# A decoder block whose activation and weight slots start at different places modulo 512 bytes

## The chip, the cores and the metric

The kernel runs on one core of a Trainium2 chip. The metric is the device time of one execution in microseconds (us). Before the change it is 3482.91 us, the median of three runs (3481.14 to 3483.26).

## The reference

One block of a hybrid decoder, 256 tokens, model width 2048, all in float32. It is cut here to what the kernel's large products compute:

```python
xn = _rms_norm(h, mix_norm_w[l])
proj = xn @ w_in[l]                       # 2048 x 26720
p_ssm, p_gdn, p_gate = jnp.split(proj, [SSM_PROJ, SSM_PROJ + GDN_PROJ], axis=-1)
y_ssm = _ssd_branch(p_ssm, ...) @ w_branch_ssm[l]      # 4096 x 2048
y_gdn = _gdn_branch(p_gdn, ...) @ w_branch_gdn[l]      # 4096 x 2048
gates = jax.nn.sigmoid(p_gate.reshape(b_, t, N_BRANCHES, D_MODEL) + gate_b[l])
mixed = gates[:, :, 0] * y_ssm + gates[:, :, 1] * y_gdn
h = h + mixed @ w_out[l]                               # 2048 x 2048
hn = _rms_norm(h, ffn_norm_w[l])
h = h + _peer_ffn(hn, peer_w_q[l], peer_sub_keys[l], peer_u[l], peer_v[l])
return _rms_norm(h, final_norm_w)
```

`_ssd_branch` and `_gdn_branch` are the two mixers, each a short convolution, gates and a chunked scan. `_peer_ffn` scores 128 x 128 single-neuron experts by product keys, takes 16 of them per head and token, and sums `gate * gelu(u . x) * v` over them.

## The kernel before

All weights pass through the core once, as a stream of 1,129 units of at most 128 x 1024 float32 values. `Stream.load` fetches a unit into one of four slots named raw, on the SP queue. `Stream.split` cuts it into two float32r parts: whi, a copy by ScalarE (line 107), and wlo, the remainder by VectorE (line 108). There are three slots for whi and three for wlo, and two units are cut ahead of the one in use.

The activations are cut in the same way into a high and a low part. They lie in the pool `act`, four slots of 16 KB per partition, all named t16 (t in the profile's rows): first x itself and its two parts xh and xl, later the sums of the branches, h and its parts hh and hl, and in the end cf, the coefficients of the expert values. yh and yl, the parts of a mixer's output, and m16 (m in the rows), the parts of the gated sum, lie in other pools, which come after the weights' slots in memory.

`product` runs one product: per chunk of 128 rows of the contraction and per block of 128 tokens three matmuls into one PSUM accumulator, high x high (line 302), high x low (line 303) and low x high (line 304). The activations are the stationary block of 128 x 128, loaded anew for each matmul, and the weights move, mostly 512 columns at a time. One product has 352 columns (`small`), one has 256. The chain of products is: the input projection tile by tile with the branch products between its tiles, the output projection, the queries of the expert layer, and `u` against all 16,384 experts. After them `mixing` (lines 1021, 1022, 1027 and 1024) multiplies the coefficients with the expert values v, 256 units of 12 matmuls, into eight accumulators, four of them named acc and four pst. All this is one fixed order, written out by the Python loops. Between the matmuls of `product`, `Background` hands out small steps of the mixers, the scoring and the gates: transpositions (line 234), small matmuls and VectorE and ScalarE work.

A float32r column is four bytes, so a stationary block takes 512 bytes of a partition, a moving half of a unit 2,048 bytes, and every chunk of a 512-column product starts a multiple of 512 bytes after its slot's start. Slots of one name follow each other without a gap, each as long as the longest tile of that name, and here all these lengths are multiples of 512.

Of the kernel before, what the change touches and what calls it, by code (L numbers as in the profile page):

```python
# [8 lines left out]
F = mybir.dt.float32  # L9
FR = mybir.dt.float32r  # L10
# [4 lines left out]
PSUM = bass.MemoryType.PSUM  # L15
DRAM = bass.MemoryType.DRAM

D = 2048
# [9 lines left out]


def in_proj_tiles():  # L30
    """Column ranges of w_in for each streamed tile, in the order in which they are used."""
    z, xs, b, c = 0, 4096, 8192, 9216
    dt = 10240
    gq, gk, gv = GDN_BASE, GDN_BASE + 2048, GDN_BASE + 4096
    gz = GDN_BASE + 8192
    bt = GDN_BASE + 12288

    def bc(g):
        return [(b + 128 * g, 128), (c + 128 * g, 128)]

    t = {"small": bc(0) + [(dt, 64), (bt, 16), (bt + 16, 16)]}
    for h in range(NH):
        t["qkv", h] = [(gq + 128 * h, 128), (gk + 128 * h, 128), (gv + 256 * h, 256)]
    for j in range(NH // 2):
        t["gz", j] = [(gz + 512 * j, 512)]
    for g in range(NG):
        t["sx", g] = [(xs + 512 * g, 512)]
        t["sz", g] = [(z + 512 * g, 512)]
    for g in (1, 3, 5):
        t["bc", g] = bc(g) + bc(g + 1)  # L50
    t["bc", 7] = bc(7)
    for i in range(2):
        for n in range(4):
            t["gate", i, n] = [(GATE_BASE + 2048 * i + 512 * n, 512)]
    return t


def schedule():
    """The order in which the weight tiles of the mixing sub-layer are used."""
    o = [("in", ("gz", 0)), ("in", "small")]  # L60
    for j in range(NH // 2):
        o.append(("in", ("qkv", 2 * j)))
        if j > 1:
            o.append(("br", "gdn", j - 2))
        o.append(("in", ("qkv", 2 * j + 1)))
        if j != 6:
            o.append(("in", ("gz", min(j + 1, 7))))
    o += [("in", ("gate", 1, 0)), ("in", ("gate", 1, 1)), ("br", "gdn", NH // 2 - 2),
          ("in", ("gate", 1, 2)), ("br", "gdn", NH // 2 - 1)]
    for g in range(NG):  # L70
        if g % 2:
            o.append(("in", ("bc", g)))
        o += [("in", ("sx", g)), ("in", ("sz", g))]
        if g:
            o.append(("br", "ssm", g - 1))
    o += [("in", ("gate", 1, 3)), ("in", ("gate", 0, 0)), ("in", ("gate", 0, 1)),
          ("br", "ssm", NG - 1), ("in", ("gate", 0, 2)), ("in", ("gate", 0, 3))]
    return o


class Stream:
    """Weights from DRAM: raw units ahead of their use, each cut into two float32r parts."""

    def __init__(self, tc, nc, ctx, units, raw_bufs, cut_bufs):
        self.nc, self.units = nc, units
# [13 lines left out]

    def split(self):  # L100
        t, n = self.raw.pop(self.ns)
        hi = self.pc.tile([128, 1024], FR, name="whi")
        lo = self.pc.tile([128, 1024], FR, name="wlo")
        step = n if self.ns else n // 2
        for c in range(0, n, step):
            s = slice(c, c + step)
            self.nc.scalar.activation(hi[:, s], t[:, s], AF.Copy)  # L107
            self.nc.vector.tensor_tensor(lo[:, s], t[:, s], hi[:, s].bitcast(F), op=OP.subtract)  # L108
        self.cut[self.ns] = (hi, lo)
        self.ns += 1  # L110
        self.load()
# [7 lines left out]


class Background:
    """Chains of small steps that run between the large products."""

    def __init__(self, cool=3):
        self.q, self.clock, self.cool = [], 0, cool
# [33 lines left out]
def block(ctx, tc, nc, I, out, dbg=None):  # L159
    cp = ctx.enter_context(tc.tile_pool(name="consts", bufs=1))  # L160
    T16 = ctx.enter_context(tc.tile_pool(name="act", bufs=4))
# [2 lines left out]
    dram = ctx.enter_context(tc.tile_pool(name="dram", bufs=1, space=DRAM))  # L164
    V, S, G, PE = nc.vector, nc.scalar, nc.gpsimd, nc.tensor

# [1 line left out]
    order = schedule()  # L168
    tiles = in_proj_tiles()
    wide = {}  # L170
    units = []
# [20 lines left out]
    for i, v in v_order:  # L192
        add_units("v", (2 * i + v) * 128 * 1024, 1, 1024)

# [1 line left out]
    def big_tile():  # L196
        return big.tile([128, 512], F, name="acc")

    def ps_tile():
        return psp.tile([128, 512], F, name="pst")  # L200

    half = cp.tile([128, 2], F, name="half")
# [12 lines left out]
    scb, snw, gnw = cols[:, 448:496], cols[:, 496:528], cols[:, 528:530]  # L215
    rows = cp.tile([128, 240], F, name="rows")

    xs = T16.tile([128, 2, D], F, name="t16")
    strm = Stream(tc, nc, ctx, units, 4, 3)
    first = ExitStack()  # L220
    xt = first.enter_context(tc.tile_pool(name="first", bufs=1)).tile([128, 16, T], F, name="xt")
# [8 lines left out]
    def power(dst, src, which, n):  # L230
        G.tensor_tensor(dst, src, half[:, which:which + 1].to_broadcast([128, n]), op=OP.pow)

    def tr(dst, src):
        PE.transpose(dst, src, ident)  # L234

# [1 line left out]
    def row_scale(r, m, parts):  # L237
        """m = sum of squares / D + eps, r = m ** -1/2, [128, 2] each"""
        V.tensor_reduce(m, parts, axis=mybir.AxisListType.X, op=OP.add)
        V.tensor_scalar(m, m, 1.0 / D, EPS, op0=OP.mult, op1=OP.add)  # L240
        power(r, m, 0, 2)
# [45 lines left out]

    accg = T16.tile([128, 2, D], F, name="t16")

# [1 line left out]
    def product(lhs, nk, w, kpu, hook=None):  # L291
        """per token block, in PSUM: the sum over k chunks of lhs(k, tb) x streamed weights"""
        ps = [big_tile() for _ in range(2)]
        for u in range(nk // kpu):
            hi, lo = strm.next()
            for a in range(kpu):
                k = u * kpu + a
                h_, l_ = hi[:, a * w:(a + 1) * w], lo[:, a * w:(a + 1) * w]
                for tb in range(2):
                    xa, xb = lhs(k, tb)  # L300
                    o = ps[tb][:, :w]
                    PE.matmul(o, xa, h_, start=k == 0, stop=False)  # L302
                    PE.matmul(o, xa, l_, start=False, stop=False)  # L303
                    PE.matmul(o, xb, h_, start=False, stop=k == nk - 1)  # L304
                if hook:
                    hook(k)
                bg.step(1)
        return ps
# [1 line left out]
    def x_lhs(k, tb):  # L310
        return xh[:, k, tb * 128:(tb + 1) * 128], xl[:, k, tb * 128:(tb + 1) * 128]

# [1 line left out]
    raw0 = cp.tile([128, 2, 352], F, name="raw0")  # L314
    dt = cp.tile([128, 2, 80], F, name="dt")
    acs = cp.tile([128, 2, 80], F, name="acs")
# [6 lines left out]
    def small_gen():  # L323
# [8 lines left out]
        al = cp.tile([128, 80], F, name="al")  # L332
        S.activation(al, rows[:, 80:160], AF.Exp)
        V.tensor_scalar(beta, beta, 0.5, 0.5, op0=OP.mult, op1=OP.add)
        # log(1 + e) = 2 atanh(e / (2 + e))
        V.tensor_scalar(s_, e_, 2.0, None, op0=OP.add)
        V.reciprocal(s_, s_)
        V.tensor_tensor(s_, s_, e_, op=OP.mult)
# [12 lines left out]
        p = ps_tile()  # L351
# [9 lines left out]
        p = ps_tile()  # L361
# [2 lines left out]
        S.activation(aux[:80, 2, 0, :T], p[:80, :T], AF.Copy)  # L364
        S.dma_start(racs.rearrange("h a b -> h (a b)"), aux[:80, 2, 0, :T])

# [1 line left out]
    mix = ExitStack()  # L368

    def conv(items, w, bias):  # L370
        """items of (dst, src psum [128, 256], chunk); dst gets half the causal convolution (+ bias)"""
        for dst, src, c in items:
            S.activation(dst, src, AF.Identity, scale=w[:, c, 3:4], bias=0.0 if bias is None else bias[:, c:c + 1])  # L373
        for k in (2, 1, 0):
            s = 3 - k
            for dst, src, c in items:
                V.scalar_tensor_tensor(dst[:, s:], src[:, :T - s], w[:, c, k:k + 1], dst[:, s:], op0=OP.mult, op1=OP.add)  # L377

    def conv_silu(pool, src, nch, chunk_of, w, bias, dst):
        """src(tb, i) [128 t, 128 c] in SBUF; dst [128 c, nch, 256] = silu(conv)"""  # L380
        y = pool.tile([128, 4, T], F, name="t4", bufs=NT4[0])
        for i0 in range(0, nch, 2):
            p = ps_tile().rearrange("p (a b) -> p a b", a=2)
            for a in range(2):
                for tb in range(2):
                    tr(p[:, a, tb * 128:(tb + 1) * 128], src(tb, i0 + a))
            conv([(y[:, i0 + a, :], p[:, a, :], chunk_of(i0 + a)) for a in range(2)], w, bias)
            yield
        th = pool.tile([128, 4, T], F, name="t4", bufs=NT4[0])
        for i0 in range(0, nch, 2):  # L390
            S.activation(th[:, i0:i0 + 2, :], y[:, i0:i0 + 2, :], AF.Tanh)
            V.scalar_tensor_tensor(dst[:, i0:i0 + 2, :], th[:, i0:i0 + 2, :], 1.0, y[:, i0:i0 + 2, :],
                                   op0=OP.add, op1=OP.mult)
# [329 lines left out]
    for o in order:  # L723
# [8 lines left out]
        t = o[1]  # L732
# [33 lines left out]
        elif t[0] == "bc":  # L766
# [4 lines left out]
            e = bg.add(bc_gen(lambda tb, i, pt=pt: pt[:, tb, i * 128:(i + 1) * 128], groups))  # L771
# [11 lines left out]
        for tb in range(2):  # L783
            nc.sync.dma_start(dbg["mixed"][tb * 128:(tb + 1) * 128, :], accs[0][:, tb, :])

# [1 line left out]
    h = T16.tile([128, 2, D], F, name="t16")  # L787
    hh = T16.tile([128, 16, T], FR, name="t16")
    hl = T16.tile([128, 16, T], FR, name="t16")
# [16 lines left out]
    for n in range(4):  # L806
# [7 lines left out]
        e = bg.add(h_gen(n))  # L814
# [10 lines left out]
    def h_lhs(k, tb):  # L825
        return hh[:, k, tb * 128:(tb + 1) * 128], hl[:, k, tb * 128:(tb + 1) * 128]

# [1 line left out]
    tv, i1f, i2f = (pp.tile([128, 2, 8, 16], F, name=n) for n in ("tv", "i1f", "i2f"))  # L829
    pos = pp.tile([128, 2, 8, 16], U32, name="pos")  # L830

# [128 lines left out]
        es.append(bg.add(score_gen(i, q)))  # L960
    ge = bg.add(gate_gen(es))

# [1 line left out]
    def act_gen(u, ps):  # L964
        a_ = pp.tile([128, 2, 512], F, name="p4", bufs=6)
        for tb in range(2):
# [9 lines left out]
            yield  # L976
        S.dma_start(hdr[u], ht)

# [1 line left out]
    def gate_load(qg, half):  # L980
        ks = slice(16 * half, 16 * half + 16)
        src = gdr[ks, :, qg * 16:qg * 16 + 16, :].rearrange("k p i t -> p k i t")
# [15 lines left out]
    for u in range(32):  # L998
# [7 lines left out]
        e = bg.add(act_gen(u, ps))  # L1006
# [45 lines left out]
    for i2, hv in v_order:  # L1052
# [11 lines left out]
        cut = strm.next()  # L1064
# [9 lines left out]
        if hv and 124 <= i2 < 126:  # L1074
            tb = i2 - 124
# [1 line left out]
            if tb == 0:  # L1077
                weigh(0)

# [1 line left out]
    residual(1, 0)  # L1081
    for i2, hv, cut in held:
        mixing(i2, hv, cut, 1)
# [75 lines left out]
```

## Time and profile before

| | before |
|---|---|
| median of the runs | 3482.91 us |
| lowest and highest run | 3481.14 and 3483.26 us |
| span of the profiled execution | 3480.8 us |
| its granted TensorE clock, mean | 0.998 |
| TensorE matmuls busy | 99% of the span, 16,598 instructions |
| VectorE busy | 66% |
| ScalarE busy | 51% |
| moved by DMA | 682.36 MB, 196 GB/s |

The span is that of the one execution that the profiler recorded, from its first to its last instruction. The profile has no other time for this execution, so the span stands for its own time; the median of the runs is 2.1 us above it, less than the spread of the runs. A busy share adds up the durations that the profiler gives, and the end of a matmul is modelled there, so that matmuls that follow each other overlap in the rows. How fast TensorE goes is read from the distance of their starts.

### The profile page before, as it was taken

Reading aid. Unit: us, or ns where it says so; the run is one execution under the profiler, and the core shown is the slowest. Engines: PE = TensorE matmul, PEld = TensorE weight load, DVE = VectorE, ACT = ScalarE, POOL = GpSimd, SP = SyncE. Lnnn points to the kernel's source line nnn. Section 1 sums busy time; section 2 is a strip of 40 time slices with the busy share of each in tenths; the row PEclk is TensorE's granted clock in tenths of the full one; section 3 lists DMA queues with packets and bytes.
Section 4 is the critical chain, followed back from the end, with each engine's and each line's share of the span. In section 5 each row is a group of like instructions: output and inputs, shape, how many; then the busy total and the mean of one; then the engine's idle time right before and its main releaser. Section 6 shows DMA issues by size and latency. Waiting matters only on the chain.

```text
span 3480.8 us, 44496 instructions
## 1 busy us (share of the span) xinstructions
PE 3449.5 (99%) x16598; PEld 2849.9 (82%) x16598; DVE 2308.9 (66%) x3262; ACT 1762.0 (51%) x2420; POOL 318.3 (9%) x262
## 2 busy tenths in 40 slices
PE   9999999999999999999999999999999999999998
PEld 7888888888878888888888888888888788888886
DVE  6675766666667677777665667768887455555555
ACT  5565555555445554544445444446666444444444
POOL 0111111111100000000000000003443000000000
PEclk9999999999999999999999999999999999999999
DMA  7544444544555555555566566666777777777774
GB/s 258 158 138 152 151 145 142 154 150 147 157 166 183 192 187 182 185 178 182 189 203 200 172 199 208 206 210 224 236 241 242 253 245 242 241 242 243 241 234 163
DMA packets 233720, 682.36 MB, mean 196 GB/s; under 512 B 21072, under 2 KB 72480, under 8 KB 233248
## 3 DMA queue, kind: packets, MB, share of 16 engines
q1 hardware_dynamic: 164960, 594.03, 53.7%
q10 hardware_dynamic: 67616, 81.31, 6.8%
q0 software_dynamic: 928, 4.19, 0.4%
q8 instruction: 130, 2.13, 0.3%
q14 instruction: 86, 0.70, 0.1%
HBM read 643.71 MB, written 35.73 MB: 195 GB/s over the span
## 4 chain that ended last, share of the span: by engine, by line
PE 69%; DVE 1%; ACT 1%; issue 0%; ACTq 0%; DMA 0%; POOL 0%; POOLq 0%; DVEq 0%
PE acc L302 15%; PE acc L304 15%; PE acc L303 15%; PE acc L1022 3%; PE acc L1021 3%; PE acc L1027 3%; PE pst L1027 3%; PE pst L1021 3%; PE pst L1022 3%; PE pst L234 2%; PE pst L948 1%; PE pst L594 1%; DVE wlo L108 0%; ACT whi L107 0%; PE pst L598 0%
## 5 line engine op out<-in xcount | busy, mean ns | idle before, releaser
L108 DVE TENSOR_TENSOR wlo<-raw,whi 128x1024 fp32r<-128x1024 f32 (+1 forms) x1129 | 1439.9, 1282 | 916.2 <-ACT whi L107 906.1
L107 ACT ACTIVATE whi<-raw 128x1024 fp32r<-128x1024 f32 (+1 forms) x1129 | 1184.9, 1053 | 850.9 <-PE acc L304 440.5
L302 PE MATMUL acc<-whi,t 128*128 128x512 f32 (+2 forms) x2848 | 1168.8, 410 | 9.7 <-ACT whi L107 9.7
L304 PE MATMUL acc<-whi,t 128*128 128x512 f32 (+2 forms) x2848 | 1110.3, 390 | 0.0
L303 PE MATMUL acc<-wlo,t 128*128 128x512 f32 (+2 forms) x2848 | 1108.0, 389 | 1.8 <-DVE wlo L108 1.8
L304 PEld LDWEIGHTS acc<-whi,t 128*128 128x128 f32 x2848 | 535.6, 188 | 115.7
L302 PEld LDWEIGHTS acc<-whi,t 128*128 128x128 f32 x2848 | 536.7, 188 | 105.1 <-ACT whi L107 10.2
L303 PEld LDWEIGHTS acc<-wlo,t 128*128 128x128 f32 x2848 | 537.6, 189 | 99.2 <-DVE wlo L108 3.9
L302 PE MATMUL acc<-whi,yh 128*128 128x512 f32 x512 | 216.8, 423 | 2.8 <-ACT yh L249 2.8
L304 PE MATMUL acc<-whi,yl 128*128 128x512 f32 x512 | 202.9, 396 | 0.0
L303 PE MATMUL acc<-wlo,yh 128*128 128x512 f32 x512 | 202.4, 395 | 0.0
L1022 PE MATMUL pst<-wlo,t 128*128 128x512 f32 x512 | 200.0, 391 | 2.1 <-DVE wlo L108 2.1
L1021 PE MATMUL pst<-whi,t 128*128 128x512 f32 x512 | 200.1, 391 | 0.0
L1021 PE MATMUL acc<-whi,t 128*128 128x512 f32 x512 | 199.2, 389 | 0.0
L1022 PE MATMUL acc<-wlo,t 128*128 128x512 f32 x512 | 199.2, 389 | 0.0
L931 POOL TENSOR_TENSOR b<-ob,gp 128x1024 f16<-128x1024 f16 x64 | 141.0, 2203 | 625.6 <-DVE ob L930 625.6
L1027 PE MATMUL pst<-whi,t 128*128 128x512 f32 x508 | 156.8, 390 | 0.0
L1027 PE MATMUL acc<-whi,t 128*128 128x512 f32 x508 | 156.4, 389 | 0.0
L377 DVE SCALAR_TENSOR_TENSOR t<-pst,cols,t 128x255 f32<-128x255 f32 x336 | 135.9, 474 | 23.7 <-ACT t L373 23.3
L302 PEld LDWEIGHTS acc<-whi,yh 128*128 128x128 f32 x512 | 96.8, 189 | 23.2 <-ACT yh L249 3.2
L304 PEld LDWEIGHTS acc<-whi,yl 128*128 128x128 f32 x512 | 96.5, 188 | 23.3 <-DVE yl L250 0.2
L1022 PEld LDWEIGHTS pst<-wlo,t 128*128 128x128 f32 x512 | 96.5, 188 | 22.5 <-DVE wlo L108 2.4
(267 smaller groups left out, 3325.8 us busy)
## 6 DMA issues: line engine op xcount, KB each, us to landing
raw<-w_in SPq DMA_DIRECT2D x408, 512.0 KB, 3.6
raw<-u SPq DMA_DIRECT2D x256, 512.0 KB, 4.0
raw<-v SPq DMA_DIRECT2D x256, 512.0 KB, 4.4
raw<-w_gdn SPq DMA_DIRECT2D x64, 512.0 KB, 3.5
raw<-w_ssm SPq DMA_DIRECT2D x64, 512.0 KB, 4.4
raw<-w_out SPq DMA_DIRECT2D x32, 512.0 KB, 3.8
raw<-w_q SPq DMA_DIRECT2D x32, 512.0 KB, 3.6
hdr<-ht ACTq DMA_DIRECT2D x32, 512.0 KB, 4.9
```

What stands on the lines that cost most here:

```text
L107: self.nc.scalar.activation(hi[:, s], t[:, s], AF.Copy)
L108: self.nc.vector.tensor_tensor(lo[:, s], t[:, s], hi[:, s].bitcast(F), op=OP.subtract)
L234: PE.transpose(dst, src, ident)
L302: PE.matmul(o, xa, h_, start=k == 0, stop=False)
L303: PE.matmul(o, xa, l_, start=False, stop=False)
L304: PE.matmul(o, xb, h_, start=False, stop=k == nk - 1)
L377: V.scalar_tensor_tensor(dst[:, s:], src[:, :T - s], w[:, c, k:k + 1], dst[:, s:], op0=OP.mult, op1=OP.add)
L594: PE.matmul(p[:, i * 64:(i + 1) * 64], sc[:, i, :], xdt[:, c, i, :], start=True, stop=True)
L931: G.tensor_tensor(b2, ob[:, None, :, :].to_broadcast([128, 2, 4, 128]), gp[:, :, ts, None].to_broadcast([128, 2, 4, 128]), op=OP.mult)
L1021: PE.matmul(o_, a, hi[:, s], start=i2 == 0, stop=False)
L1022: PE.matmul(o_, a, lo[:, s], start=False, stop=False)
L1027: PE.matmul(acc[tb][2 * hv + n], b, hi[:, n * 512:(n + 1) * 512], start=False, stop=False)
```

## The change

Three tiles get longer rows: whi 1,040 float32 values for 1,024, wlo 1,072, and x in its t16 slot 4,112 for 4,096. Only the first 1,024 or 4,096 are used. As all slots of a name have the length of its longest tile, all four t16 slots are 64 bytes longer, the whi slots 64 and the wlo slots 192. What comes after them in memory moves up, by 256 bytes for raw and whi and by 1,024 for the pools behind. Comments and descriptions in the file are taken out as well; lines keep their numbers.

```diff
     def split(self):
         t, n = self.raw.pop(self.ns)
-        hi = self.pc.tile([128, 1024], FR, name="whi")
-        lo = self.pc.tile([128, 1024], FR, name="wlo")
+        hi = self.pc.tile([128, 1040], FR, name="whi")
+        lo = self.pc.tile([128, 1072], FR, name="wlo")
...
-    xs = T16.tile([128, 2, D], F, name="t16")
+    xs = T16.tile([128, 2 * D + 16], F, name="t16")[:, :2 * D].rearrange("p (a b) -> p a b", a=2)
```

Where the slots start, in bytes modulo 512, as the two programs are built (in order of address):

| slots | before | after |
|---|---|---|
| t16, four | 320, 320, 320, 320 | 320, 384, 448, 0 |
| raw, four | 320 each | 64 each |
| whi, three | 320 each | 64, 128, 192 |
| wlo, three | 320 each | 256, 448, 128 |
| m16, two | 320 | 320 |
| yh and yl in the delta mixer | 192 | 192 |
| yh and yl in the SSM mixer | 384 | 384 |

The t16 slots hold in turn, in the same order of address: xh, the scoring keys, staged gates and cf; a store of gates, the SSM branch's sum and hl; x, the delta branch's sum and hh; xl and h. The instructions of each engine stand in the same order before and after.

## The prediction

> **What bounds the kernel now.** I read the page first, then the waits of TensorE, then the groups with their shapes kept apart, then TensorE's instructions in order of time in a few quiet stretches.
>
> ```profile
> span 3480.8 us, 44496 instructions
> PE 3449.5 (99%) x16598; PEld 2849.9 (82%) x16598; DVE 2308.9 (66%) x3262; ACT 1762.0 (51%) x2420; POOL 318.3 (9%) x262
> PE 69%; DVE 1%; ACT 1%; issue 0%; ACTq 0%; DMA 0%; POOL 0%; POOLq 0%; DVEq 0%
> ...
> PE acc L302 <- ACT whi L107: 9.7, 2, 6.8
> PE pst L1022 <- DVE wlo L108: 2.1, 1, 2.1
> PE acc L303 <- DVE wlo L108: 1.8, 3, 0.8
> ```
>
> TensorE is busy for 99% of the span and waits on the cutting of weights (L107, L108) for hardly 14 us in all. So the time is the number of matmuls times the distance from one start to the next, and a change that reorders nothing can only act through that distance, or by making another engine so slow that TensorE waits. The durations below overlap, since a matmul's modelled end lies behind the start of the next; the distance has to be read from start times.
>
> ```profile
> L302 PE MATMUL acc<-whi,t 128*128 128x512 f32 x2784 | 1149.1, 413 | 9.7 <-ACT whi L107 9.7
> L304 PE MATMUL acc<-whi,t 128*128 128x512 f32 x2784 | 1090.9, 392 | 0.0
> L303 PE MATMUL acc<-wlo,t 128*128 128x512 f32 x2784 | 1088.7, 391 | 1.8 <-DVE wlo L108 1.8
> ...
> L302 PE MATMUL acc<-whi,yh 128*128 128x512 f32 x512 | 216.8, 423 | 2.8 <-ACT yh L249 2.8
> L304 PE MATMUL acc<-whi,yl 128*128 128x512 f32 x512 | 202.9, 396 | 0.0
> L303 PE MATMUL acc<-wlo,yh 128*128 128x512 f32 x512 | 202.4, 395 | 0.0
> ...
> L1021 PE MATMUL acc<-whi,t 128*128 128x512 f32 x512 | 199.2, 389 | 0.0
> L1022 PE MATMUL acc<-wlo,t 128*128 128x512 f32 x512 | 199.2, 389 | 0.0
> L1027 PE MATMUL acc<-whi,t 128*128 128x512 f32 x508 | 156.4, 389 | 0.0
> ...
> L302 PE MATMUL acc<-whi,m 128*128 128x512 f32 x128 | 50.7, 396 | 0.0
> L303 PE MATMUL acc<-wlo,m 128*128 128x512 f32 x128 | 50.0, 391 | 0.1
> L304 PE MATMUL acc<-whi,m 128*128 128x512 f32 x128 | 49.9, 390 | 0.0
> ```
>
> All of these are the same operation, 512 columns of float32r weights against a 128x128 stationary block, and yet those with yh and yl take 395 to 396 ns where the value stage (L1021 to L1027, whose three groups have twins of the same counts that write pst) takes 389. What tells them apart is the place in memory. In the built program before, every slot of t, m, whi and wlo starts 320 bytes after a multiple of 512, and every step inside a slot that a 512-column product takes is a multiple of 512 too; yh and yl alone start at 192 (delta mixer) or 384 (SSM mixer). So the trace of before already holds both cases of the change: matmuls whose two TensorE streams (the moving weights, and the stationary block that is loaded beside them for the next matmul) start at the same remainder, and matmuls where they do not. Two neighbouring stretches of undisturbed matmuls, first the input product of a gate, then the SSM branch:
>
> ```profile
> 1703.05 0.39 PE L302 MATMUL acc<-whi,t 128*128 128x512 f32 x1
> ...
> 1736.83 0.39 PE L304 MATMUL acc<-whi,t 128*128 128x512 f32 x1
> ...
> 1738.20 0.40 PE L304 MATMUL acc<-whi,yl 128*128 128x512 f32 x1
> ...
> 1759.43 0.39 PE L302 MATMUL acc<-whi,yh 128*128 128x512 f32 x1
> ```
> ```profile
> 1703.44:1737.04 33.60, 33.60 (x150) 27.81 (x149) 17.61 (x16) 14.28 (x14) 0.54 (x1) 1.00 0.67 213
> 1738.36:1759.65 21.29, 21.29 (x92) 17.14 (x92) 13.59 (x15) 9.32 (x9) 0.00 (x0) 1.00 0.60 194
> 2800.00:2900.00 100.00, 100.00 (x443) 82.81 (x442) 55.09 (x46) 42.71 (x41) 0.00 (x0) 1.00 0.75 246
> ```
>
> The second fence gives length, TensorE's busy time and count, and near the end the granted clock, 1.00 in all three. A window counts each matmul that reaches into it, so the first count runs from the start at 1703.05 to that at 1736.83: 33.78 us for 149 steps, 226.7 ns each. The second runs from 1738.20 to 1759.43: 21.23 us for 91 steps, 233.3 ns. The value stage has about (100 + 0.39) / 443 = 226.6 ns. So at full clock, with nothing waiting, **equal remainders cost 226.7 ns and unequal ones 233.3**, 6.6 ns or 2.9% more, and the SSM remainder (64 ahead) and the delta remainder (128 behind, rows below, alternately 0.24 and 0.23 or less) agree on the mean.
>
> ```profile
> 998.38 0.39 PE L304 MATMUL acc<-whi,yl 128*128 128x512 f32 x1
> 998.61 0.40 PE L302 MATMUL acc<-whi,yh 128*128 128x512 f32 x1
> 998.85 0.39 PE L303 MATMUL acc<-wlo,yh 128*128 128x512 f32 x1
> ...
> 1003.04 0.39 PE L303 MATMUL acc<-wlo,yh 128*128 128x512 f32 x1
> ```
>
> From 998.38 to 1003.04 the rows are 20 steps: 4.66 / 20 = 233 ns.
>
> **The change part by part.** No instruction moves: the order on each engine is the same. What moves is where slots start. T16 slots go from 320 throughout to 320, 384, 448 and 0; whi to 64, 128, 192 over its three buffers; wlo to 256, 448, 128; raw to 64; yh, yl and m keep theirs. Of 12,657 pairs of a 512-column matmul and a following one whose block is loaded beside it, 11,236 have equal remainders before and 137 after; the rest spread over all seven multiples of 64, most of them (3,685) at 256.
>
> Value stage. 512 x 4 + 508 x 2 = 3,064 matmuls, already at the settled pace, go from 226.7 to 233.3: 3,064 x 6.6 ns = 20.2 us. Its edge matmuls (L1024, 8 of them) are left out.
>
> Products with t and m. 3 x 2,784 + 3 x 128 = 8,736 matmuls. They are not all at the settled pace now: after each background transposition or small matmul the distance starts anew near 231 to 236 ns and settles within about ten matmuls, which is why L303 and L304 stand at 391 and 392 and not at 389. The yh and yl groups, which have such interruptions too, stand at 395 and 396. The difference by line is 395 - 391 and 396 - 392, 4 ns each. L302 shows 423 - 413 = 10, but that line comes first after each interruption, and the delta branch has many; I take 4 there too. 8,736 x 4 = 34.9 us.
>
> Products with yh and yl, 1,536 matmuls: unequal before and after, 0. If the new remainder were free there, -1,536 x 6.6 = -10 us; if it cost once more, +10. Both ends go into the range.
>
> Sum: +55.1 us on TensorE, all of it on the path, as nothing else bounds. Six of the seven differences other than zero are seen only in part: 64 and 384 have a price in the rows, the others have none. Bounds: from below, the shortest distance that comes back in the trace, 224 ns, just after an interruption, first two rows here; from above, the longer of the delta branch's alternating distances, 998.61 to 998.85, 0.24 us.
>
> ```profile
> 1014.48 0.39 PE L304 MATMUL acc<-whi,t 128*128 128x512 f32 x1
> 1014.70 0.39 PE L302 MATMUL acc<-whi,t 128*128 128x512 f32 x1
> ...
> L108 DVE TENSOR_TENSOR wlo<-raw,whi 128x1024 fp32r<-128x1024 f32 x1111 | 1425.3, 1290 | 907.5 <-ACT whi L107 897.5 <-PE acc L304 8.0
> L107 ACT ACTIVATE whi<-raw 128x1024 fp32r<-128x1024 f32 x1111 | 1172.6, 1058 | 839.0 <-PE acc L304 428.9 <-PE acc L1027 156.9 <-PE pst L1027 153.9
> ```
>
> At 224 for all 11,800 matmuls: -2.7 x 11,800 = -32 us. At 240: +13.3 x 3,064 + (240 - 231) x 8,736 = 41 + 79 = +120 us. I take 233.3, the mean at both remainders that have a row.
>
> VectorE and ScalarE read and write the moved slots as well. A unit's cut is 1.06 + 1.29 = 2.35 us, and the value stage consumes a unit in 12 x 226.7 = 2.72 us; whichever way the remainders move these, a slowdown under 0.37 us (16%) stays under the matmuls, since two units are cut ahead, and a speedup shortens only idle time (907 us before L108). I cost both at 0; past those 16%, each further 0.1 us in the 256 units of the value stage would be 26 us. The DMA into raw is four units deep and its engines are busy for 0.60 to 0.75 of these windows: 0 likewise.
>
> One rule speaks against all this. The Trainium skill, SBUF — State Buffer, "Who interferes with whom", gives TensorE two independent read ports, one for the moving operand and one for the load, lets engines contend on the port pair of VectorE and GpSimd alone, and says PE and ACT never wait on anyone; by it the remainders would be worth 0 us where the rows above make +55. The trace disagrees as far as two paces at one clock go (226.7 and 233.3 ns), but it cannot show that the remainder is their cause.
>
> **The rivals.** *Nothing changes (3483).* The slower pace of yh and yl could come from something else about them: they are the only stationary tiles at the top of the memory, past 207,000 bytes, where t and m lie below 170,000. Then every other product keeps its pace. For it speaks the one product of 352 columns, whose second half of each unit starts 128 bytes off the stationary slot's remainder:
>
> ```profile
> 43.00 0.32 PE L302 MATMUL acc<-whi,t 128*128 128x352 f32 x1
> ...
> 43.95 0.33 PE L302 MATMUL acc<-whi,t 128*128 128x352 f32 x1
> ...
> 44.91 0.32 PE L302 MATMUL acc<-whi,t 128*128 128x352 f32 x1
> ```
>
> Six steps unequal in 0.95 us, six equal in 0.96: 158 and 160 ns, no loss. Against it: at 352 columns the moving stream ends 384 bytes from where it began, so that its "equal" half isn't in step from matmul to matmul either.
>
> *Faster.* What settles at 226.7 may itself contain a collision of two streams that start together, and a well chosen offset may avoid it; the 352-column rows lean that way by 1%. From the lowest row, 224 ns, the price is the -32 us above: 3451. It decides once the mean over all differences falls under about 226 in the settled stretches. Against it: both offsets with a row at 512 columns are slower. The Trainium skill, TensorE: Matmul & The Clock Gate, "Wait — 56ns, not 53.3ns?", has 215.7 ns start to start at 512 columns; if that were reached, 11 x 13,336 matmuls = 147 us would go, an estimate from that page that no row here shows.
>
> *Slower by less.* If only the remainder modulo 256 mattered, the 3,685 pairs at 256 would keep their pace: 55 x (1 - 3,685 / 12,520) = 39 us, 3522. *Slower by more.* The moving stream now jumps in remainder between hi and lo at each matmul, which no row shows; at 240 ns it is 3603.
>
> **How the numbers follow.** The profiled span is 3480.8 us, the median of the runs 3482.9, 2.1 us more; 3480.8 + 55.1 + 2.1 = 3538. Chances: slower near the forecast, the partial form included, 0.66; slower by far more 0.06; nothing 0.11; faster 0.17. A measurement can tell about 0.2% (7 us) from no change. The range reaches from 3470, which takes in no change and the smallest gains, to 3600; outside lie most of the faster case and about half of the far slower one. Within the likeliest case alone I would say 3515 to 3560.
>
> **What would show it.** Right: the value stage's 100 us windows count near 430 matmuls for 443, L1021 to L1027 stand at 395 to 396, L303 and L304 with t at the same; yh and yl stay; VectorE still waits for ScalarE before L108. Wrong: groups at 389 as before (then it is the place of yh and yl, not the remainder), under 389 (the faster case), or TensorE waiting on L107 and L108 for much over 14 us, which would be the cut and not the pace.

## The result and the profile after

The change makes the kernel slower: 3519.03 us median of four runs (3518.33 to 3519.3) against 3482.97, a ratio of 1.0105 with a 95% interval of 1.0091 to 1.012. That is 36 us more; 3538 was forecast, in a range of 3470 to 3600.

The page after, and the waits of TensorE:

```profile
span 3517.1 us, 44496 instructions
PE 3487.1 (99%) x16598; PEld 2847.9 (81%) x16598; DVE 2310.7 (66%) x3262; ACT 1761.9 (50%) x2420; POOL 305.9 (9%) x262
...
PE acc L302 <- ACT whi L107: 8.5, 2, 6.4
PE pst L1022 <- DVE wlo L108: 2.1, 1, 2.1
...
PE acc L303 <- DVE wlo L108: 1.7, 3, 0.8
```

TensorE is still busy for 99% of a span that is 36.3 us longer, with as many instructions, and its waits on the cut are no longer than before. So no other engine came into play; the same matmuls take longer. The groups with their shapes kept apart say which (last column but one: mean ns of one), and one window of 100 us in the value stage gives the pace:

```profile
L302 PE MATMUL acc<-whi,t 128*128 128x512 f32 x2784 | 1155.3, 415 | 8.5 <-ACT whi L107 8.5
L303 PE MATMUL acc<-wlo,t 128*128 128x512 f32 x2784 | 1101.1, 396 | 1.7 <-DVE wlo L108 1.7
L304 PE MATMUL acc<-whi,t 128*128 128x512 f32 x2784 | 1096.4, 394 | 0.0
...
L302 PE MATMUL acc<-whi,yh 128*128 128x512 f32 x512 | 216.0, 422 | 2.0 <-ACT yh L249 2.0
...
L303 PE MATMUL acc<-wlo,yh 128*128 128x512 f32 x512 | 201.5, 394 | 0.0
L1021 PE MATMUL acc<-whi,t 128*128 128x512 f32 x512 | 201.5, 394 | 0.0
L304 PE MATMUL acc<-whi,yl 128*128 128x512 f32 x512 | 201.3, 393 | 0.0
L1027 PE MATMUL acc<-whi,t 128*128 128x512 f32 x508 | 159.3, 394 | 0.0
```
```profile
2850.00:2950.00 100.00, 100.00 (x433) 80.99 (x432) 52.84 (x44) 41.79 (x41) 0.00 (x0) 1.00 0.73 237
```

In the value stage the groups that write acc go from 389 to 394 ns, and 3,064 x 5 = 15 us; 433 matmuls reach into 100 us where 443 did, (100 + 0.4) / 433 = 231.9 ns from start to start for 226.7. In the products with t, L302, L303 and L304 gain 2, 5 and 2 ns; by their busy times 24.1 us. m adds 1 us, and yh and yl give back 3 us. That makes 37 us against the 36.3 measured. The clock in the window is 1.00, as before.

### The profile page after: what moved, and what is told of

It reads as the page before. It is cut to its first block, busy times and chain, and to the rows that moved or that the text cites. A ratio compares the mean times of both kernels' runs of the same rounds, so it can differ in the third digit from the quotient of the medians.

```text
span 3517.1 us, 44496 instructions
## 1 busy us (share of the span) xinstructions
PE 3487.1 (99%) x16598; PEld 2847.9 (81%) x16598; DVE 2310.7 (66%) x3262; ACT 1761.9 (50%) x2420; POOL 305.9 (9%) x262
## 4 chain that ended last, share of the span: by engine, by line
PE 97%; DVE 1%; ACT 1%; issue 1%; DMA 0%; ACTq 0%; POOL 0%; POOLq 0%; SPq 0%; DVEq 0%
PE acc L302 22%; PE acc L303 22%; PE acc L304 22%; PE pst L234 3%; PE acc L1022 3%; PE acc L1021 3%; PE acc L1027 3%; PE pst L1022 3%; PE pst L1027 3%; PE pst L1021 3%; PE pst L470 1%; PE pst L478 1%; PE pst L948 1%; PE pst L594 1%; DVE wlo L108 1%
## 5 line engine op out<-in xcount | busy, mean ns | idle before, releaser
L302 PE MATMUL acc<-whi,t 128*128 128x512 f32 (+2 forms) x2848 | 1174.9, 413 | 8.5 <-ACT whi L107 8.5
L303 PE MATMUL acc<-wlo,t 128*128 128x512 f32 (+2 forms) x2848 | 1120.5, 393 | 1.7 <-DVE wlo L108 1.7
L304 PE MATMUL acc<-whi,t 128*128 128x512 f32 (+2 forms) x2848 | 1115.8, 392 | 0.0
L304 PEld LDWEIGHTS acc<-whi,t 128*128 128x128 f32 x2848 | 535.3, 188 | 122.5
L302 PEld LDWEIGHTS acc<-whi,t 128*128 128x128 f32 x2848 | 536.9, 189 | 113.7 <-ACT whi L107 9.0
L303 PEld LDWEIGHTS acc<-wlo,t 128*128 128x128 f32 x2848 | 537.9, 189 | 104.9 <-DVE wlo L108 3.8
L302 PE MATMUL acc<-whi,yh 128*128 128x512 f32 x512 | 216.0, 422 | 2.0 <-ACT yh L249 2.0
L303 PE MATMUL acc<-wlo,yh 128*128 128x512 f32 x512 | 201.5, 394 | 0.0
L304 PE MATMUL acc<-whi,yl 128*128 128x512 f32 x512 | 201.3, 393 | 0.0
L931 POOL TENSOR_TENSOR b<-ob,gp 128x1024 f16<-128x1024 f16 x64 | 130.7, 2043 | 646.6 <-DVE ob L930 646.6
L1021 PEld LDWEIGHTS pst<-whi,t 128*128 128x128 f32 x512 | 96.0, 188 | 22.9 <-ACT whi L107 0.3
L304 PEld LDWEIGHTS acc<-whi,yl 128*128 128x128 f32 x512 | 96.2, 188 | 22.6 <-DVE yl L250 0.2
```

The source lines that it names most:

```text
L931: G.tensor_tensor(b2, ob[:, None, :, :].to_broadcast([128, 2, 4, 128]), gp[:, :, ts, None].to_broadcast([128, 2, 4, 128]), op=OP.mult)
L1021: PE.matmul(o_, a, hi[:, s], start=i2 == 0, stop=False)
```

## Experiments

Theory A: the pace depends on the difference, modulo something, between where the moving weights and the stationary block start. Theory B: it costs that the moving stream jumps between hi and lo. The first four runs are compared with the kernel before at 3482.04 us, its median in runs taken beside theirs.

**All slots moved alike.** `warm` gets 17 values for 1, so that everything behind it moves by 64 bytes.

```diff
-    warm = cp.tile([128, 1], F, name="warm")
+    warm = cp.tile([128, 17], F, name="warm")[:, :1]
```

> Every slot (t16, raw, whi, wlo, m16, yh, yl) is moved by the same 64 bytes, to 384 modulo 512 where it was 320; the differences between slots stay as before. If the difference between the two streams of TensorE counts (theory A), nothing changes: 3483 us within 3, 226.7 ns per matmul in the value stage. If the place itself counts (a good and a bad remainder), up to the +36 us of the change appear.

Measured: 3483.0 us, ratio 1.0003 (0.9994 to 1.0012). So a shift of 64 bytes that all slots share costs nothing; what counts is how they lie to each other.

**The activations alone.** The line for xs from the change, whi and wlo as before.

> Only the activations' slots are lengthened: t16 at 320, 384, 448 and 0, while whi and wlo agree with each other (64 throughout). 376 equal pairs are left of 11236. Theory A (the difference between the moving stream and the stationary block loaded beside it): about the whole of the change, +30 to +55 us, value stage at 231 to 234 ns. Theory B (it costs that the moving stream jumps between hi and lo, which here it does not): 0 to +10 us, value stage at 226.7 ns.

Measured: 3497.09 us, ratio 1.0047 (1.0033 to 1.0061), 15 us more, between what A and B gave. The reason shows in the value stage, whose stationary cf now lies 256 bytes from whi and wlo, and in the products with t:

```profile
L302 PE MATMUL acc<-whi,t 128*128 128x512 f32 x2784 | 1154.5, 415 | 9.1 <-ACT whi L107 9.1
L304 PE MATMUL acc<-whi,t 128*128 128x512 f32 x2784 | 1095.7, 394 | 0.0
L303 PE MATMUL acc<-wlo,t 128*128 128x512 f32 x2784 | 1094.8, 393 | 1.7 <-DVE wlo L108 1.7
...
L1021 PE MATMUL acc<-whi,t 128*128 128x512 f32 x512 | 199.3, 389 | 0.0
L1022 PE MATMUL acc<-wlo,t 128*128 128x512 f32 x512 | 199.2, 389 | 0.0
L1027 PE MATMUL acc<-whi,t 128*128 128x512 f32 x508 | 156.5, 389 | 0.0
```

The value stage kept 389 ns, the pace of equal places. So either 256 counts as equal, or B; but the products with t lost 2 ns a matmul although the moving stream did not jump there, which B does not allow. What they lost, 2,784 x (2 + 2 + 2) = 17 us, is the whole difference and a little more; yh and yl give 2 us back.

The group means hide how much a settled stretch loses. In the input product, whi and wlo lie 256 bytes from xh and 64 from xl, so one stationary block in three is out of place:

```profile
1709.01 0.40 PE L302 MATMUL acc<-whi,t 128*128 128x512 f32 x1
...
1738.82 0.40 PE L302 MATMUL acc<-whi,t 128*128 128x512 f32 x1
```

These are 129 steps in 29.81 us, 231.1 ns each where the same product took 226.7 before. By the start times, the steps after L302, L303 and L304 take 233.2, 231.0 and 229.0 ns: one block out of place slows all three.

**The cut weights alone.** The lines for hi and lo from the change, xs as before.

> Only whi and wlo are lengthened: whi at 320, 384, 448, wlo at 0, 192, 384, t16 all at 320. One slot of whi in three still agrees with t16, 2502 equal pairs are left of 11236. Theory A: 0.78 of the change, +25 to +36 us. Theory B (jumps of the moving stream): the whole, +36 us or more. So together with the run on the activations alone: A expects both large and their sum well over 36, B expects this one alone to be large.

Measured: 3513.03 us, ratio 1.0091 (1.0078 to 1.0105), 31 us more: inside what A expected. With the run before it makes 46 us, more than both together (36), so the two halves of the change do not add up; B alone would have had the first at zero.

**yh and yl moved to the same place as the rest.** In both mixers yh gets unused values ahead of it, 32 or 112, which brings yl behind it to 320 as well.

```diff
-        yref += [mx.tile([128, 4, T], FR, name=n, bufs=1) for n in ("yh", "yl")]
+        yref += [mx.tile([128, 4 * T + 112], FR, name="yh", bufs=1)[:, 112:].rearrange("p (a b) -> p a b", a=4),
+                 mx.tile([128, 4, T], FR, name="yl", bufs=1)]
```

> The kernel before with yh and yl moved to 320 modulo 512, by 32 and 112 unused values ahead of yh, at the same top end of the memory; all 12657 pairs are equal then. Theory A: the yh and yl groups fall from 395 to 391 or 389 ns, 1536 x 4 to 6.6 ns = 6 to 10 us less, 3473 to 3477 us. If their slower pace came from their place at the top of the memory or from what runs beside them: 3483 us.

Measured: 3476.71 us, ratio 0.9987 (0.9978 to 0.9996), 5 us under the kernel before. The groups, and rows of an SSM branch, which ran at 233.3 ns before:

```profile
L302 PE MATMUL acc<-whi,yh 128*128 128x512 f32 x512 | 214.8, 420 | 2.8 <-ACT yh L249 2.8
L304 PE MATMUL acc<-whi,yl 128*128 128x512 f32 x512 | 200.7, 392 | 0.0
L303 PE MATMUL acc<-wlo,yh 128*128 128x512 f32 x512 | 200.3, 391 | 0.0
```
```profile
1733.41 0.39 PE L302 MATMUL acc<-whi,yh 128*128 128x512 f32 x1
...
1753.35 0.39 PE L303 MATMUL acc<-wlo,yh 128*128 128x512 f32 x1
```

From start to start 19.94 us for 88 steps, 226.6 ns. The tiles are at the same top end of the memory, the work beside them is the same; only the remainder moved. This settles the rival that yh and yl were slow for their place. 512 x (3 + 4 + 4) ns = 5.6 us is the gain.

**A sweep over the difference.** Units of the value stage are cut into longer slots at an offset that grows by 16 bytes every 8 units.

```diff
-        hi = self.pc.tile([128, 1024], FR, name="whi")
-        lo = self.pc.tile([128, 1024], FR, name="wlo")
+        hi = self.pc.tile([128, 1152], FR, name="whi")
+        lo = self.pc.tile([128, 1152], FR, name="wlo")
+        v = self.ns - (len(self.units) - 256)
+        oh, ol = (4 * (v // 8), 4 * (v // 8)) if v >= 0 else (0, 0)
+        hi, lo = hi[:, oh:oh + 1024], lo[:, ol:ol + 1024]
```

> The kernel before, but in the value stage whi and wlo start 16 bytes further every 8 units (0, 16, ... 496 bytes past 320), both alike; the stationary cf stays at 320. Each step is 96 matmuls, of which the last 60 or so are settled. If the remainder counts modulo 256 (theory A, amended after the run on the activations alone, whose value stage lay 256 apart and kept 226.7 ns): 226.7 ns at offsets 0 and 256, 231 to 234 ns over most of the others, the second half a copy of the first, the stage 13 to 20 us longer. If only jumps of the moving stream cost (theory B): 226.7 ns throughout. If some offset avoids a collision that 226.7 still contains: below 226 ns there.

Measured (one run, 3498.94 us): the rows of two steps, offsets 160 and 256, first and last start of 57 settled distances each (lines 1024 and 1025 of this kernel are 1021 and 1022 of the one before):

```profile
3000.86 0.39 PE L1024 MATMUL pst<-whi,t 128*128 128x512 f32 x1
...
3014.21 0.40 PE L1025 MATMUL pst<-wlo,t 128*128 128x512 f32 x1
...
3134.39 0.39 PE L1024 MATMUL pst<-whi,t 128*128 128x512 f32 x1
...
3147.31 0.39 PE L1025 MATMUL pst<-wlo,t 128*128 128x512 f32 x1
```

13.35 / 57 = 234.2 and 12.92 / 57 = 226.7 ns. All steps in that way, from the start times in the trace:

| offset of the moving weights, bytes | 0 | 16 | 32 | 48 | 64 | 80 | 96 | 112 |
|---|---|---|---|---|---|---|---|---|
| ns per matmul | 226.7 | 231.7 | 233.3 | 233.4 | 228.9 | 231.1 | 233.3 | 231.1 |
| the same 256 bytes further | 226.7 | 231.7 | 233.3 | 233.4 | 228.9 | 231.1 | 233.3 | 231.1 |

| offset, bytes | 128 | 144 | 160 | 176 | 192 | 208 | 224 | 240 |
|---|---|---|---|---|---|---|---|---|
| ns per matmul | 232.5 | 233.3 | 234.2 | 231.1 | 233.3 | 234.7 | 233.4 | 226.7 |
| the same 256 bytes further | 232.5 | 233.3 | 234.2 | 231.1 | 233.3 | 234.7 | 233.4 | end of the stage |

The second half repeats the first: the period is 256 bytes, not 512. No offset is under 226.7, so the faster rival falls for these matmuls of 512 columns. Only 0 and 240 keep that pace, the mean of the 16 is 231.8, and within a step the moving stream did not jump between hi and lo, so B alone falls too.

**hi and lo apart.** The same with `16 * (v // 64), 16 * (v // 16 % 4)` for the two offsets, and with `0, 4 * (v // 8)`.

> The same, with whi 0, 64, 128 or 192 bytes past 320 (64 units each) and inside of that wlo 0, 64, 128 or 192 past it (16 units, 192 matmuls each). Theory A alone, each matmul priced by its own difference to the block loaded beside it: 226.7 for (0, 0), 228.9 where only wlo is off (two of six matmuls), 231 where only whi is off (four of six), 233 where both are. Theory A and B together: the diagonal is cheaper than its neighbours, and (0, x) costs more than 229.

> The same with whi left at 320 and wlo alone 16 bytes further every 8 units. Theory A: 226.7 ns at 0 and 256, near 229 elsewhere (two of six matmuls at 233). With a price on jumps as well: 230 to 235 ns in places, again with a period of 256.

Measured (3497.24 and 3496.18 us, one run each), settled ns per matmul from the start times of the first:

| whi off by | wlo 0 | wlo 64 | wlo 128 | wlo 192 |
|---|---|---|---|---|
| 0 | 226.7 | 232.8 | 230.0 | 231.9 |
| 64 | 232.2 | 228.9 | 232.8 | 231.1 |
| 128 | 230.6 | 232.2 | 232.3 | 233.4 |
| 192 | 228.9 | 231.8 | 232.2 | end of the stage |

The sums of single prices fail: with wlo alone off by 64, two matmuls of six, 228.9 was expected and 232.8 came; the run that moves wlo alone lies at 230.0 to 233.3 between offsets 16 and 224, at 228.9 at 240, and at 226.7 only at 0 and 256. A matmul out of place slows its neighbours too: in that step no distance is under 228 ns. Nor is the diagonal always the cheapest of its row. The pace belongs to the whole repeating pattern.

**The change with 256 bytes.** xs, hi and lo get 64 unused values each.

```diff
+    xs = T16.tile([128, 2 * D + 64], F, name="t16")[:, :2 * D].rearrange("p (a b) -> p a b", a=2)
...
+        hi = self.pc.tile([128, 1088], FR, name="whi")
+        lo = self.pc.tile([128, 1088], FR, name="wlo")
```

> The change with 256 bytes in place of its 64, 64 and 192: t16 at 320, 64, 320, 64, whi at 320, 64, 320 and wlo at 64, 320, 64 modulo 512, so that slots lie at two places modulo 512 but all at one modulo 256; 4119 pairs are 256 apart and the moving stream jumps by 256 at each matmul. If what counts has a period of 256, as the sweep of one stage says: 3482 us within 3, value stage 226.7 ns. If it is 512, or if the jump itself costs: +20 us or more.

Measured: 3481.83 us against 3481.91, ratio 1.0 (0.9991 to 1.0009); in the value stage 443 matmuls in 100 us:

```profile
2900.00:3000.00 100.00, 100.00 (x443) 82.84 (x442) 56.25 (x47) 43.48 (x42) 0.00 (x0) 1.00 0.72 236
```

Jumps of 256 bytes at each matmul cost nothing, over the whole program.

**The stationary operand alone.** cf is moved by 96 bytes in its slot.

```diff
-            cf = T16.tile([128, 2, 2, 4, T], FR, name="t16")
+            cf = T16.tile([128, 16 * T + 128], FR, name="t16")[:, 24:24 + 16 * T].rearrange("p (s q i t) -> p s q i t", s=2, q=2, i=4)
```

> The kernel before with cf alone, the stationary operand of the value stage, moved up by 96 bytes in its slot (t16 slots 512 bytes longer, all other remainders as before; raw, whi and wlo agree). If only the difference between the stationary block and the moving weights counts, this is the sweep's offset of 160 (96 the other way, modulo 256): 234.2 ns settled, about 3050 x 7.6 = 23 us more, near 3505. If the sweep's cost came from whi and wlo standing apart from raw, for the engines that cut: 226.7 ns and 3482.

Measured: 3505.43 us (one run), 23.5 more than the 3481.91 of before. In the same 100 us:

```profile
2900.00:3000.00 100.00, 100.00 (x429) 80.38 (x428) 53.21 (x45) 40.92 (x39) 0.00 (x0) 1.00 0.73 236
```

(100 + 0.40) / 429 = 234.0 ns, close to the sweep's 234.2 for an offset of 160. raw, whi and wlo agree here, so the cost is TensorE's own, not that of the engines that cut.

**The transpositions' identity at 320 as well**, with yh and yl as above: `cst` starts 32 values into a longer tile.

> The kernel with yh and yl at 320, and the identity that the transpositions stream at 320 as well (192 before). If the state in which an interruption leaves the two streams depends on that remainder, the ten or so matmuls that settle after each interruption change, up to 30 us either way of 3476.7; if it depends on time alone, 3476.7 within 3.

Measured: 3475.52 us, ratio to before 0.9983 (0.9974 to 0.9992), its span 3475.5 against 3475.0 without this step: nothing more is gained. How TensorE settles after an interruption does not hang on this step of the identity's remainder to a measurable degree. The two kernels with yh and yl in place are the fastest here.

## Why the prediction was right, and where not

*What bounds.* Right: the distance between matmuls was the only thing that moved the time. VectorE's cut went from 1290 to 1298 ns a unit and stayed covered, as costed.

*Equal against unequal remainder.* Right, and shown: yh and yl brought to the same remainder ran at 226.6 ns in place of 233.3, and cf taken off it at 234.0 in place of 226.7.

*The modulus.* Wrong in the forecast, right in a rival: equal modulo 256 is enough. "Slower by less" gave 3522 for it, and 3519 came, but only by compensation: the 3,685 pairs at 256, 29% of those that no longer start alike, did not keep their pace after the change, since the moving stream jumped by 64, 192 or 320 between hi and lo around them. They do keep it where whi and wlo agree modulo 256. A unit of the value stage after the change whose whi lies 256 bytes from cf and whose wlo lies 448, from its first matmul to that of the next unit:

```profile
2868.23 0.40 PE L1021 MATMUL acc<-whi,t 128*128 128x512 f32 x1
...
2871.02 0.39 PE L1021 MATMUL pst<-whi,t 128*128 128x512 f32 x1
```

Twelve steps in 2.79 us are 232.5 ns each. By the start times, units of this kind take 232.6 ns a matmul on the mean, and the two other kinds, with nothing at 0 or 256, take 231.5 and 231.4: the units with pairs at 256 are the dearest.

*The price, 233.3 ns at all remainders.* This is the step that was mis-sized. The two remainders with a row before lie on the dear side (the sweep has 232.5 and 233.3 for them, and 231.8 as a mean). In the value stage 6.6 ns a matmul was taken and 231.9 - 226.7 = 5.2 came, so that its term of 20 us measured 15 to 16. With t and m 4 ns was taken and 2.9 came (24.1 us over 8,352 matmuls with t): 35 us measured 25. yh and yl were put at 0 and gave 3 back. Together 55 became 37.

*Pace and the page's rule.* The Trainium skill, SBUF — State Buffer, "Who interferes with whom", has the moving read and the weight load on independent ports, and TensorE never waiting on anyone. These runs differ: the same matmuls take 226.7 to 234.7 ns by the places of their two operands alone. That it is a port or a bank which the two share is not shown; only the period and the price are.

*The faster rival.* Its floor of 224 ns was not held as a pace: no settled step of the three runs with offsets has a mean under 226.7 ns. Where 224 comes back in them, with wlo off by 144 for example, it stands between longer distances, and the mean is 231.

*The 352-column rows.* They showed a limit of the rule that the prediction did not draw. The change moved the slots under the two narrow products as well, and neither got slower. The 352-column groups stand at 322 to 323 ns before and after, and the 256-column product became a little faster; first two rows before, then after:

```profile
1589.04 0.28 PE L302 MATMUL acc<-whi,t 128*128 128x256 f32 x1
...
1595.40 0.28 PE L304 MATMUL acc<-whi,t 128*128 128x256 f32 x1
```
```profile
1594.00 0.28 PE L302 MATMUL acc<-whi,t 128*128 128x256 f32 x1
...
1600.28 0.28 PE L304 MATMUL acc<-whi,t 128*128 128x256 f32 x1
```

Each is 53 steps, 120.0 ns before and 118.5 after; in the run on the activations alone it is 117.7, and in the one with 256 bytes 120.0 again. So the price was seen with 512 columns alone. Why the width matters is open.

## What to carry to other kernels

Where TensorE is the bound and streams float32r 512 columns at a time, start the stationary and the moving operands, hi and lo parts alike, at the same remainder modulo 256 bytes, and look at the built addresses of every tile, since small tiles ahead in a pool push the later ones off. Spreading slots over remainders to avoid collisions did the opposite here. When a trace of before has the same operation at two paces, look for what differs between their operands before predicting. And where it shows two cases of many, take their price as a sample: both may lie on the dear side, as here, and one run that sweeps the offsets gives the others.

## What the runs showed of the hardware that was not expected

- The period is 256 bytes. In steps of 16 bytes, the moving stream 16 behind the stationary one's remainder (offset 240) is free, 226.7 ns, and 16 ahead of it costs 5.0 ns a matmul.
- The price isn't monotonous: 228.9 ns at an offset of 64, 234.7 at 208.
- Prices don't add: the activations alone cost 15 us, the weights alone 31, both 36.
- At 256 columns the sign turns: 120.0 ns at equal remainders, 117.5 to 118.5 where the change or half of it is in.
- Left open: whether the block being loaded or the one in use sets the pace against the moving stream. In the runs with offsets both had the same remainder; where they differ, in the input product with the activations alone moved, all three steps get longer, so it does not tell them apart either.
